# Seven products in place of eight for sixteen blocks of the down projection, and an opening in four parts, in a hybrid decoder step

## The chip, the cores and the metric

The kernel runs on one core of a Trainium2 chip. The time is that of one execution on the device, in microseconds (us); the profile adds one execution recorded instruction by instruction. The engines are PE (TensorE, matmuls), PEld (its weight load, which overlaps PE), DVE (VectorE), ACT (ScalarE), POOL (GpSimd) and SP (SyncE, which issues most DMAs). Each engine works through its own instructions in order, and semaphores make one wait for another.

## What is computed

One layer of a hybrid decoder for 1024 prompt tokens and 8 sample tokens, with 1024 channels: three mixers read the same normalized input through one combined projection, their outputs are merged into the residual, and a SwiGLU network with 2816 hidden channels follows. Cut to what matters here:

```python
xn = rmsnorm(x, norm_mix_w)
sc_b, sc_c, sc_x, z, xbc, dt_raw, q, gates = jnp.split(xn @ w_in, splits, axis=-1)
...
x = x + merged @ w_merge_o
hn = rmsnorm(x, norm_ffn_w)
x = x + (jax.nn.silu(hn @ w_ffn_gate) * (hn @ w_ffn_up)) @ w_ffn_down
y = rmsnorm(x, final_norm_w)
```

(The last lines are written here in short form.) Besides y, the step returns keys and values of the memory and the new convolution and state-space states.

## The kernel before

All activations lie channels by tokens: a tile is 128 channels by 1032 tokens (1024 prompt, 8 sample), and the halves of a tile are 516 tokens. Each number is split into a rounded high part and the rest (`hi` by a cast on ACT, `lo` by a subtraction on DVE), and a product is three matmuls: high·high, low·high, high·low. There are two ways to multiply. `gemm` (L183–206) takes a weight block of 128 columns against whole tiles in three pieces of 344 tokens. `strassen` (L290–350) takes two weight blocks at once and the input channels in two halves, and uses Strassen's identity: seven products of half-size operands in place of eight. For it the activations must lie in seven forms (B11, T1, nT2, B21, T3, B22, T4), each made of halves of the tiles by additions; the sums of weights are made by DVE per call. It works in three PSUM tiles of 516 tokens in two banks (m0, m1, m2), in matmuls of 258 tokens (L248). The products of a call come in the order B11, T1, nT2, B21, T3, B22, T4; a finished one is evacuated by an ACT copy (L318, L326, L329) or added by DVE (L331, L342, L344).

The program runs in stages on one core:

- **Opening** (L400–553): three groups of three token tiles (384 tokens; the last with the sample). For each group the mean square of each token (`square`, ACT), its root (`root_of`, DVE and PE), then per channel tile the transposes on PE into PSUM, an ACT copy to `xt` that SP stores to `xT_d` (the residual), the scaling on DVE into `xw`, and the split into `xn`. The products of the first two weight blocks (wB0, wC0) with a group run while the next group is prepared (`first_products` L500–502), and `step_sizes` gives dt. SP's queue carries, in this order: three token tiles, eight small parameter loads into `rows`, the weights wB0, wC0, wdt, the bias, the other token tiles.
- **z and Strassen forms**: two z blocks by `gemm`, the forms of xn (L1128–1145), then pairs of blocks by `strassen` (Z2 to Z14, G16, X17 to X19, and so on). Small work is put between products by a list `pend`, one entry per `tick`.
- **State-space scan, attention, output projections, merge** (untouched by the change).
- **Gate and up** (L1813–1845): the 22 hidden blocks in pairs (0, 1), (2, 3), and so on, each pair one `strassen` call for gate and one for up, then Silu and product, and SP stores each hidden tile to `h_d`.
- **Down** (L1869–1884): blocks 0–2, then 3–10, then 11–18 by `gemm`: `hidden` loads a tile of `h_d` and splits it, eight output tiles are computed per group, and DVE adds each to `x2[m]`, which was loaded from `x2_d` ahead. Blocks 19–21 belong to the finish, which goes token piece by token piece (L2003–2020) with the last norm and the output.

What stands on an engine's queue is decided by a scheduler that orders the instructions, by tile pools (a tile waits until the buffer that it takes is free), and by the few explicit `issue_after`.

## Time and profile before

| what | us |
|---|---|
| median of three timed runs | 2490.22 (2489.02 to 2492.35) |
| the profiled execution | 2485.14 |
| its span in the trace | 2483.4 |
| opening, to the first z product | 0 to 65.2 |
| last gate/up call (u20) | 2195.34 to 2215.6 |
| down projection, blocks 0 to 18 | 2216.44 to 2432.6 |
| finish | 2432.6 to 2483.4 |

The profiled execution lies 5.1 us below the median of the timed runs. In the opening PE is busy for 0.73 us of the first ten, then for 7.2, 7.5, 7.7 and 9.0 of each ten up to 50, and fully from there. To read rows of a timeline: start, duration, engine, line, operation, output<-inputs, shapes, and in brackets how long the engine was idle before it and what ended that.

### The profile page before, as it was taken

What the parts mean: (1) busy time and instruction counts of PE and PEld (TensorE: products, weight loads), DVE (VectorE), ACT (ScalarE), POOL (GpSimd) and SP (SyncE); (2) the same over time, 40 slices, a digit from 0 to 9 for tenths busy, and PEclk for the clock granted to TensorE, in tenths of its full rate; (3) what the DMA queues carried; (4) which work ended last, traced back from release to release, by engine and by line L of the source; (5) the groups of instructions that cost most, each with busy time, mean ns of one, the idle gap of its engine ahead of it and who ended that gap; (6) DMA issues with size and microseconds to landing.
All of it is one profiled execution on the core that took longest, in us unless ns stands there. A gap on an engine that the chain in (4) does not pass through costs nothing.

```text
span 2483.4 us, 44787 instructions
## 1 busy us (share of the span) xinstructions
PE 2442.8 (98%) x18691; PEld 2377.6 (96%) x18691; DVE 1505.5 (61%) x2434; ACT 1056.5 (43%) x1700; POOL 119.1 (5%) x163
## 2 busy tenths in 40 slices
PE   7999999999999999999999999999999999999998
PEld 5999999999999999999899988999999999999998
DVE  5744576786777676568677763555775544463315
ACT  5733554555453543656554442223443233341203
POOL 0200000000000000112211000000000000000000
PEclk9999999999999999999999999999999999999999
DMA  6444323444353345667886886855443222273211
GB/s 196 144 154 153 121 86 112 129 136 129 111 155 116 104 129 181 214 223 260 259 281 219 261 319 235 289 162 175 133 154 101 88 70 93 69 253 123 77 35 69
DMA packets 348474, 392.08 MB, mean 158 GB/s; under 512 B 15350, under 2 KB 285798, under 8 KB 348263
## 3 DMA queue, kind: packets, MB, share of 16 engines
q1 hardware_dynamic: 327678, 331.23, 42.6%
q10 hardware_dynamic: 20593, 57.97, 6.1%
q8 instruction: 147, 2.41, 0.4%
q14 instruction: 56, 0.46, 0.1%
HBM read 280.40 MB, written 108.98 MB: 157 GB/s over the span
## 4 chain that ended last, share of the span: by engine, by line
PE 89%; DMA 5%; DVE 3%; ACT 1%; issue 1%; SPq 0%; ACTq 0%; DVEq 0%; POOL 0%
PE po L203 11%; PE pd L203 9%; PE pm L1742 4%; PE ps_q L203 2%; PE pss L966 1%; PE py L953 1%; DMA qb<-qs_d 1%; PE X17m L248 1%; PE po L945 1%; PE ps_z L203 1%; PE Z2m L248 1%; PE G16m L248 1%; PE X4m L248 1%; PE X8m L248 1%; PE C7m L248 1%
## 5 line engine op out<-in xcount | busy, mean ns | idle before, releaser
L1884 DVE TENSOR_TENSOR x<-pd,x 128x1032 f32<-128x1032 f32 x24 | 29.5, 1231 | 129.3 <-PE pd L203 129.3
L898 ACT ACTIVATE r<-r,acum 128x128 f32<-128x128 f32 x256 | 78.9, 391 | 6.0 <-DMA r<-ac_d 5.5
L680 DVE SCALAR_TENSOR_TENSOR ax<-u,prm,ax 128x1024 f32<-128x1024 f32 x44 | 56.3, 1280 | 0.0
L839 ACT ACTIVATE st<-st,es 128x128 f32<-128x128 f32 x128 | 41.3, 392 | 24.8 <-DMA st<-in_state_ssm_dram 14.0
L930 POOL TENSOR_TENSOR xdd<-xdt,decst 128x512 f32<-128x512 f32 x32 | 36.2, 1131 | 280.3 <-DVE xdt L926 280.3
L924 DVE TENSOR_TENSOR r<-r,cbm 128x1024 f32<-128x1024 f32 x32 | 39.1, 1222 | 2.4 <-ACT r L899 0.4
L841 DVE SCALAR_TENSOR_TENSOR st<-sr,dts,st 128x128 f32<-128x128 f32 x128 | 40.0, 344 | 0.4
L949 DVE TENSOR_TENSOR y<-po,ea 128x512 f32<-128x512 f32 x28 | 19.3, 688 | 28.2 <-PE po L945 28.2
L845 DVE SCALAR_TENSOR_TENSOR sr<-st,sr 128x128 f32<-128x128 f32 x128 | 35.2, 284 | 1.1
L966 PE MATMUL pss<-xdd,bT 128*128 128x512 f32 x64 | 34.2, 616 | 1.1 <-ACT bT L923 0.9
L953 PE MATMUL py<-r,xdt 128*64 128x128 f32 x512 | 35.0, 279 | 0.0
L899 ACT ACTIVATE r<-r 128x1024 f32<-128x1024 f32 x32 | 33.9, 1058 | 0.6
L979 POOL TENSOR_TENSOR s<-s,cdec 128x512 f32<-128x512 f32 x28 | 33.1, 1183 | 2.6 <-DVE s L972 2.4
L1749 DVE TENSOR_TENSOR x<-pm,xT 128x516 f32<-128x516 f32 x16 | 11.1, 695 | 36.4 <-PE pm L1742 36.3
L1375 DVE TENSOR_TENSOR yr<-po,yr 128x1032 f32<-128x1032 f32 x8 | 9.8, 1231 | 38.2 <-PE po L203 38.2
L953 PEld LDWEIGHTS py<-r,xdt 128*64 128x64 f32 x512 | 27.3, 136 | 4.2 <-issue 0.6
L923 ACT COPY bT<-bp 128x128 f32<-128x128 f32 x32 | 8.5, 266 | 53.2 <-DVE cbm L921 53.0
L945 PE MATMUL po<-bc,s 128*128 128x128 f32 x224 | 29.8, 276 | 0.0
L945 PEld LDWEIGHTS po<-bc,s 128*128 128x128 f32 x224 | 28.2, 191 | 0.6 <-DVE s L972 0.4
L1476 DVE SCALAR_TENSOR_TENSOR kc<-kc,qb 128x256 f32<-128x256 f32 x64 | 23.5, 420 | 8.2 <-DMA qb<-qs_d 8.2
L1671 DVE TENSOR_TENSOR gt<-po,gt 128x1032 f32<-128x1032 f32 x8 | 9.9, 1231 | 30.7 <-PE po L203 27.1
L683 DVE SCALAR_TENSOR_TENSOR ax<-u,prm,ax 128x1032 f32<-128x1032 f32 x22 | 28.3, 1286 | 0.0
(9294 smaller groups left out, 8888.1 us busy)
## 6 DMA issues: line engine op xcount, KB each, us to landing
r<-ac_d SPq DMA_DIRECT2D x32, 512.0 KB
gt_d<-G ACTq DMA_DIRECT2D x24, 516.0 KB
gt<-gt_d SPq DMA_DIRECT2D x24, 516.0 KB
xs_d<-ax ACTq DMA_DIRECT2D x22, 516.0 KB
hr<-h_d SPq DMA_DIRECT2D x22, 516.0 KB
x<-xs_d SPq DMA_DIRECT2D x16, 516.0 KB
zs<-zs_d SPq DMA_DIRECT2D x16, 516.0 KB
yb_d<-x SPq DMA_DIRECT2D x16, 516.0 KB
```

What stands on the lines that cost most here:

```text
L203: PE.matmul(ps[:, n, :CW], wt[:, ks], x[:, n * CW : (n + 1) * CW], start=(k == 0 and i == 0), stop=(k == nk - 1 and i == 2),)
L248: PE.matmul(ps[:, n, :HC], wt[:, ks], x[:, n * HC : (n + 1) * HC], start=(start and kt == 0 and i == 0), stop=(kt == 3 and i == 2), skip_g ...
L680: V.scalar_tensor_tensor(acc[:, :T], u[:, j : j + T], w[j], acc[:, :T], op0=ALU.mult, op1=ALU.add)
L839: S.activation(st[:, i], st[:, i], AF.Copy, scale=es[:, g * 4 + i, b : b + 1])
L841: V.scalar_tensor_tensor(st[:, i], rb, dts[:, g * 4 + i, b : b + 1], st[:, i], op0=ALU.mult, op1=ALU.add)
L898: S.activation(r[:, j, :], r[:, j, :], AF.Relu, scale=-1.0, bias=acum[:, c, h : h + 1])
L924: V.tensor_tensor(r, r, bc(cbm.unsqueeze(1), [P, HPG, P]), op=ALU.mult)
L930: G.tensor_tensor(b3(xdd, HPG), b3(xdt, HPG), bc(decst[:, c, hs].unsqueeze(2), [P, HPG, 64]), op=ALU.mult)
L945: PE.matmul(po[:, t * P : (t + 1) * P], state["s"][:, t * P : (t + 1) * P], bcg[1][:, cs], start=True, stop=True,)
L953: PE.matmul(py[hp : hp + 64, (h // 2) * P : (h // 2 + 1) * P], xdt[:, h * 64 : (h + 1) * 64], r[:, (h % 2) * 4 + h // 2, :], start=True, s ...
L966: PE.matmul(pss, bT, xdd, start=True, stop=True)
L1742: PE.matmul(ps[:, n, :HC], wt[:, ks], x[:, half * HT + n * HC : half * HT + (n + 1) * HC], start=(k == 0 and i == 0), stop=(k == KD - 1 an ...
```

## The change

It has three parts.

**Down projection.** The hidden blocks are paired anew: (0, 9), (1, 5) to (4, 8), (11, 15) to (14, 18), (10, 19), (20, 21). For the eight pairs (j, j+4), DVE makes T1, T2, T3 and T4 right after the product of gate and up, and SP stores the seven half-width forms to `hf_d` in place of two tiles to `h_d`. In the down projection blocks 1–8 (part 0) and 11–18 (part 1) are then four `strassen` calls each (d00 to d06, d10 to d16), two output tiles a call. With `add=True`, `put` adds a finished product onto `x2` on DVE where ACT copied it. `st_begin` makes the weight sums of each part's first call ahead. Block 0 runs ahead of part 0, blocks 9 and 10 ahead of part 1, in halves of 516 tokens, in the same three PSUM tiles. Block 0's result is copied by ACT as the start of `x2`; the residual is loaded and added by ticks of part 0. The PSUM pool of `gemm` comes back only behind part 1.

**Opening.** Four parts of two token tiles (256, 256, 256 and 264 tokens) in place of three groups; channel tiles in the order 0, 4, 1, 5, 2, 6, 3, 7, two in one PSUM tile for the first three parts, so one evacuation of 512 columns for two; `xt` has four buffers and is stored from ACT's queue. The three weight loads follow the first two token tiles; the eight rows of the mixer norm are loaded apart from ACT's queue, the other parameters later. The square of the second tile is made by DVE. The accumulated first blocks leave PSUM in two pieces.

**Order between opening and gates.** T1 and nT2 of the forms are made before the z blocks, T4 after them; the convolutions of the two first blocks move from ahead of z into the call Z2 (`plain3`); the transposes of the memory become ticks; the first history becomes a tick of the z blocks and the other three come in the ticks of Z14, where two of them came in the last tick of G16; `bc_rows` becomes a tick.

```diff
+        def put(o, ps):
+            if add:
+                V.tensor_tensor(h3(o), hv(ps), h3(o), op=ALU.add)
+            else:
+                S.copy(h3(o), hv(ps))
...
-            S.copy(h3(o11), hv(pa))
+            put(o11, pa)
...
-        S.copy(h3(o22), hv(pb))
+        put(o22, pb)
...
-            S.copy(h3(o12), hv(pa))
+            put(o12, pa)
...
+        def tokens(g, ks):
+            n = parts[g][1]
+            ps = sm_ps(f"ps_xt{g}{ks[0]}")
+            for i, k in enumerate(ks):
+                turn(g, ps, i * n, lambda _, t, m: t[:, k * P : (k + 1) * P])
+            xt = p0.tile([P, 512], F32, tag="xt", bufs=4, name=f"xt{g}{ks[0]}")
+            S.copy(xt[:, : len(ks) * n], ps[:, : len(ks) * n])
+            to = xT_d[ks[0] :: 4] if len(ks) > 1 else xT_d[ks[0] : ks[0] + 1]
+            S.dma_start(to[:, :, part(g)].rearrange("k p t -> p k t"), b3(xt[:, : len(ks) * n], len(ks)))
+            for i, k in enumerate(ks):
+                ins = to_xn(g, k, ps[:, i * n : (i + 1) * n])
...
-    xbc_tile(16, "B0", ps_b0)
-    xbc_tile(20, "C0", ps_c0)
-    make_forms(0)
-    make_forms(2)
-    pend.extend([None, mem_rms])
+    mem_rms()
+    make_forms()
+    pend.extend([dt_turn, lambda: history("state_ssm_conv", h_xc, 16, ev_tile("hist", (24, D)))])
     z_step(0)
     z_step(1)
-    mem_block(0)
-    pend.extend([None, lambda: mem_block(1)])
+    make_forms4()
+    pend.extend([None, lambda: mem_block(0), lambda: mem_block(1)])
...
     def plain3():
         for kt in range(4):
             split_to(*xforms["T3"][kt], raw3[kt // 2][:, HS[kt % 2]])
+        xbc_conv(16, firsts[0], "B0")
+        xbc_conv(20, firsts[1], "C0")
...
+        V.tensor_sub(t1, b12, b11)
+        V.tensor_sub(t2, t1, b22)
+        V.tensor_sub(t3_, b22, b12)
+        V.scalar_tensor_tensor(t4, t2, -1.0, b21, op0=ALU.mult, op1=ALU.subtract)
+        for f, t in enumerate((b11, t1, t2, b21, t3_, b22, t4)):
+            SY.dma_start(hf_d[f, n - 1], t)
...
+    def down_pairs(part, fs, begun):
+        for m in range(0, KD, 2):
+            pa = strassen(
+                *down_src(part, m), fs, f"d{part}{m}", ev_sums,
+                lambda m=m: tuple(x2[m + i][:, c] for i in range(2) for c in HS), add=True,
+                begun=begun if m == 0 else None,
+            )
+            o21 = h3(x2[m + 1][:, HS[0]])
+            V.tensor_tensor(o21, o21, pa, op=ALU.subtract)
```

Three places show what moves. SP's queue at the program's start, before (x_ is a token tile, rows the parameter tile, wB0r to wdtr the raw weights):

```order
L405 DMA x_153<-in_x_prompt_dram 128x1024
L432 DMA rows<-in_norm_mem_w_dram 8x128
L432 DMA rows<-in_norm_mix_w_dram 8x128
L432 DMA rows<-in_norm_ffn_w_dram 8x128
L432 DMA rows<-in_sc_conv_w_dram 24x128
L432 DMA rows<-in_ssm_conv_b_dram 24x128
L432 DMA rows<-in_ssm_norm_w_dram 16x128
L432 DMA rows<-in_ssm_conv_w_dram 40x128
L432 DMA rows<-in_ssm_conv_w_dram 56x128
L124 DMA wB0r<-in_w_in_dram 128x8x128
L124 DMA wC0r<-in_w_in_dram 128x8x128
L124 DMA wdtr<-in_w_in_dram 128x8x128
```

The weight loads stand behind the third token tile and the eight parameter loads. The same queue after, from its first row:

```order
L428 DMA x_150<-in_x_prompt_dram 128x1024
L428 DMA x_152<-in_x_prompt_dram 128x1024
L124 DMA wB0r<-in_w_in_dram 128x8x128
L124 DMA wC0r<-in_w_in_dram 128x8x128
L124 DMA wdtr<-in_w_in_dram 128x8x128
L428 DMA x_160<-in_x_prompt_dram 128x1024
L428 DMA x_162<-in_x_prompt_dram 128x1024
L428 DMA x_164<-in_x_prompt_dram 128x1024
L428 DMA x_166<-in_x_prompt_dram 128x1024
```

The weights now stand behind two token tiles, and the parameters behind all of them. DVE at the first call of X17, before (ps_h is PE's transposed history, X17r the call's raw weights, sa, S and T its sums and their low parts):

```order
L660 COPY dts<-ps_ex 128x128
L661 COPY es<-ps_ex 128x128
L662 COPY dpar<-ps_ex 128x16
L550 COPY h_xc<-ps_h_8_3361 128x192
L550 COPY h_sc<-ps_h_0_3373 128x128
L315 TENSOR_TENSOR X17sa<-X17r_3422 128x512
L331 TENSOR_TENSOR u_3426<-X17m_3428,u_3426 128x516
L316 TENSOR_TENSOR X17sa<-X17sa,X17r_3420 128x512
L282 SCALAR_TENSOR_TENSOR X17sb<-X17sa,X17r_3420 128x512
L236 TENSOR_TENSOR X17Sl<-X17sa,X17Sh 128x1024
```

After, at the same place (the L754 and L757 rows are a convolution on 8 sample tokens):

```order
L736 COPY dts<-ps_ex 128x128
L737 COPY es<-ps_ex 128x128
L738 COPY dpar<-ps_ex 128x16
L337 TENSOR_TENSOR X17sa<-X17r_3504 128x512
L754 TENSOR_SCALAR ax_3709<-h_xc,prm 128x8
L338 TENSOR_TENSOR X17sa<-X17sa,X17r_3502 128x512
L757 SCALAR_TENSOR_TENSOR ax_3709<-h_xc,prm,ax_3709 128x8
L285 SCALAR_TENSOR_TENSOR X17sb<-X17sa,X17r_3502 128x512
L757 SCALAR_TENSOR_TENSOR ax_3709<-h_xc,prm,ax_3709 128x8
L239 TENSOR_TENSOR X17Sl<-X17sa,X17Sh 128x1024
```

The two history copies are gone from between dpar and X17sa. DVE where the first groups of the down projection begin, before (h7l to h10l are low parts of hidden tiles, wd02l to wd06l of weights, pd the PSUM tile of an output tile):

```order
L1866 TENSOR_TENSOR wd04l<-wd02r,wd04h 128x768
L1910 MEMSET fst 128x18
L163 TENSOR_TENSOR h7l<-hr_24146,h7h 128x1032
L163 TENSOR_TENSOR h8l<-hr_24152,h8h 128x1032
L1884 TENSOR_TENSOR x_0_23850<-pd_23872,x_0_23850 128x1032
L1884 TENSOR_TENSOR x_1_23852<-pd_23901,x_1_23852 128x1032
L1866 TENSOR_TENSOR wd06l<-wd03r,wd06h 128x768
L163 TENSOR_TENSOR h9l<-hr_24158,h9h 128x1032
L1884 TENSOR_TENSOR x_2_23854<-pd_23936,x_2_23854 128x1032
L163 TENSOR_TENSOR h10l<-hr_24164,h10h 128x1032
```

And after, at the first call d00 (B22, T3 and T4 with a digit pair are forms of part 0, d00r raw weights, L318 the adds of `put`, d00m PSUM tiles):

```order
L377 TENSOR_TENSOR T302al<-T_24195,T302ah 128x1032
L377 TENSOR_TENSOR B2200al<-B_24201,B2200ah 128x1032
L284 TENSOR_TENSOR d00sb<-d00r_24026,d00r_24028 128x512
L377 TENSOR_TENSOR B2202al<-B_24207,B2202ah 128x1032
L377 TENSOR_TENSOR T400al<-T_24213,T400ah 128x1032
L377 TENSOR_TENSOR T402al<-T_24219,T402ah 128x1032
L318 TENSOR_TENSOR x_0_24041<-d00m_24225,x_0_24041 128x516
L285 SCALAR_TENSOR_TENSOR d00sb<-d00sa,d00r_24026 128x512
L318 TENSOR_TENSOR x_1_24058<-d00m_24226,x_1_24058 128x516
L239 TENSOR_TENSOR d00Tl<-d00sb,d00Th 128x1024
L318 TENSOR_TENSOR x_0_24041<-d00m_24225,x_0_24041 128x516
L239 TENSOR_TENSOR d00Dl<-d00r_24028,d00Dh 128x512
```

In place of one add of a whole tile there are adds of halves, and the first of them stands behind the splits of the last forms.

More of the change, by code (lines that the diff above doesn't have):

```diff
@@ L434, in tile_kernel @@
                 at += m
-        ps = sm_ps("ps_prm")
-        for b in range(2):
-            PE.transpose(ps[:, b * P : (b + 1) * P], rows[:, b, :], ident)
-        V.tensor_copy(prm, ps[:, :208])
         def par(key, i):
             return prm[:, PC[key] + i : PC[key] + i + 1]
-        w_b0 = weights(wblock(w_in, C_XBC + 16 * P), "wB0")
-        w_c0 = weights(wblock(w_in, C_XBC + 20 * P), "wC0")
-        w_dt = load_raw(wblock(w_in, C_DT), "wdt")
         bias = cn.tile([P, 1], F32, tag="bias", name="bias")
@@ L460, in to_xn, with part, turn @@
+        def part(g):
+            c0, n = parts[g]
+            return slice(c0, c0 + n)
+        def turn(g, ps, at, of):
+            for i, (t, n) in enumerate(srcs[g]):
+                PE.transpose(ps[:, at + i * P : at + i * P + n], of(i, t, n), ident[:n, :n])
+        def to_xn(g, k, ps):
             hi, lo = xn[k]
-            xt = p0.tile([P, 384], F32, tag="xt", bufs=3, name="xt" + name)
-            S.copy(xt[:, :n], ps[:, :n])
-            SY.dma_start(xT_d[k, :, c], xt[:, :n])
+            c = part(g)
@@ new lines, in tile_kernel, with others, first_weights @@
+        order = (0, 4, 1, 5, 2, 6, 3, 7)
+        def others():
+            ps = sm_ps("ps_prm")
+            for b in range(2):
+                PE.transpose(ps[:, b * P : (b + 1) * P], rows[:, b, :], ident)
+            V.tensor_copy(prm[:, :200], ps[:, :200])
+        def first_weights(ins):
+            ws = []
+            for name in ("wB0", "wC0"):
+                raw = loaded.pop(name)
+                hi = wp.tile([P, 1024], F32R, tag="whi", name=name + "h")
+                in_turn("hi", S.copy(hi, raw))
+                ws.append((raw, hi))
+            for raw, hi in ws:
+                lo = wp.tile([P, 1024], F32R, tag="wlo", name="wl")
+                with tc.issue_after(ins):
+                    in_turn("lo", V.tensor_sub(lo, raw, f32(hi)))
+                yield hi, lo
@@ L497, in first_products @@
+        def first_products(g, k):
+            c, n = part(g), parts[g][1]
             ah, al = xn[k]
@@ L1898, in tile_kernel @@
+    pst_stack.close()
+    st_stack.close()
+    pmm[0] = ctx.enter_context(tc.tile_pool(name="pmm3", bufs=2, space=PSUM))
+    fin = ctx.enter_context(tc.tile_pool(name="fin", bufs=1))
+    js = list(range(19, 22))
+    for j in js:
+        hs[j] = hidden(j)
     wd = []
```

356 lines of the change are left out of this document (215 added, 141 removed).

## The prediction

> **What bounds the kernel now.** I read the page first: the busy times, the slices with the granted clock, the chain that ended last.
>
> ```profile
> span 2483.4 us, 44787 instructions
> PE   2442.8 (98%) x18691; PEld 2377.6 (96%) x18691; DVE 1505.5 (61%) x2434; ACT 1056.5 (43%) x1700; POOL 119.1 (5%) x163
> ...
> PEclk9999999999999999999999999999999999999999
> ...
> PE 89%; DMA 5%; DVE 3%; ACT 1%; issue 1%; SPq 0%; ACTq 0%; DVEq 0%; POOL 0%
> ```
>
> PE (TensorE) is busy for 98% of the span at a full granted clock, and the chain lies on PE for 89%. So there are two ways to gain: take products away from PE, or fill the 40 us in which it stands still. Where it stands still, the list of PE's waits says (line, what it waited for, total, times, longest):
>
> ```profile
> PE ps_prm L437 <- DMA rows<-in_ssm_conv_w_dram: 9.0, 1, 9.0
> PE ps_xt L481 <- DVE xw L465: 6.0, 4, 2.5
> ...
> PE X17m L248 <- ACT X17Sh L235: 2.6, 1, 2.6
> ...
> PE Z2m L248 <- ACT z L770: 1.2, 1, 1.2
> ...
> PE pd L203 <- DVE g20o L1843: 0.9, 1, 0.9
> ```
>
> The change touches each of these five places. In the chain, the end of gate and up and the down projection read so (start, duration, what):
>
> ```profile
> 2154.89 20.23 PE u18m L248 x168
> ...
> 2195.34 20.24 PE u20m L248 x168
> 2215.60 0.71 DVE g20o L1843
> 2216.44 216.12 PE pd L203 x1368
> ```
>
> A seven-product block is 168 matmuls of 258 columns in 20.23 us without a gap: 0.1204 us each. The down projection of blocks 0 to 18 is 1368 matmuls of 344 columns in 216.12 us: 0.158 us each. Both are limited by PE alone, so fewer columns are time.
>
> **Down projection, PE.** Eight blocks the old way are 8 blocks × 8 output tiles × 3 products × 3 column pieces = 576 matmuls, × 0.158 = 91.0 us. The new way is four seven-product calls, 4 × 20.23 = 80.9 us. Two such parts: 2 × (80.9 − 91.0) = **−20.2 us**. Blocks 0, 9 and 10 go in halves, 288 matmuls of 258 columns, × 0.1204 = 34.7 us, against 216 × 0.158 = 34.1: **+0.6**. The swap of PSUM pools moves behind part 1; it cost 0.9 us on L1843 and will cost about that again on the last subtraction: **0** (−0.9 to +0.9).
>
> **Down projection, what must keep up.** Evacuation moves from ACT copies to DVE adds, and forms are loaded rather than whole blocks. Rows nearest to the new operations:
>
> ```profile
> L1749 DVE TENSOR_TENSOR x<-pm,xT 128x516 f32<-128x516 f32 x16 | 11.1, 695 | 36.4 <-PE pm L1742 36.3
> L1884 DVE TENSOR_TENSOR x<-pd,x 128x1032 f32<-128x1032 f32 x24 | 29.5, 1231 | 129.3 <-PE pd L203 129.3
> ```
> ```profile
> 2103.34 0.69 DVE L236 TENSOR_TENSOR g16Dl<-g16r,g16Dh 128x512 fp32r<-128x512 f32 x1 [4.55 <-ACT g16Dh L235]
> ...
> 2113.03 1.22 DVE L236 TENSOR_TENSOR u16Sl<-u16sa,u16Sh 128x1024 fp32r<-128x1024 f32 x1
> ```
> ```profile
> 2097.15 0.59 ACT L318 COPY g16o<-g16m 128x516 f32<-128x516 f32 x1 [2.10 <-PE g16m L248]
> ...
> 2219.44 1.05 ACT L162 CAST h8h<-hr 128x1032 fp32r<-128x1032 f32 x1 [0.77 <-DMA hr<-h_d]
> ...
> 2229.25 1.06 ACT L162 CAST h9h<-hr 128x1032 fp32r<-128x1032 f32 x1 [3.64 <-DMA hr<-h_d]
> ```
>
> DVE per call: seven adds on 516 columns × 0.695 = 4.9; five operations on 512 columns × 0.69 = 3.5; three splits of 1024 × 1.22 = 3.7; together 12.0 us, in part 0 with two residual adds of 1032 × 1.23 = 14.5, of 20.23. It is not a bound by its sum. But DVE works in order, and the product that reuses a PSUM bank starts 5.78 us into a call (after B11 and T1, each 24 × 0.1204 = 2.89). At the start of the first call, three splits of forms (B22 of blocks 2 and 3, both T4) stand on DVE ahead of the first add, and the buffer of the first of them is free only as block 0's product ends. ACT then needs three casts × 1.05 = 3.15, the last split 1.23, the add 0.70, and on ACT one or two copies (0.59) come before: 5.1 to 6.3 us against 5.78, and the loads of these forms come late in a queue that already made h9 wait 3.64. I take **+1.2** (0 if all is early; 4.2 if the last form also waits for its load as h9 did: 6.3 + 3.64 − 5.78). In the other seven calls the adds are ready within 2.89 us: **0** (to 2.35 each, below). During block 0, ACT has 16 copies and four casts, 16 × 0.59 + 4 × 1.05 = 13.6 at face value, less as consecutive ACT rows overlap by about 0.1 (11.6), beside 96 × 0.1204 = 11.6 of PE: balanced, **0** (to +2, on the same bound).
>
> **Gate and up** get four DVE operations of 516 columns per pair, 2.8 us of a pair's 40.5, and store seven half pieces for two whole tiles. The row at 2103.34 shows DVE idle for 4.55 us within one block, so it is hidden: **0**; uncovered it would be 8 × 2.8 = 22. Within u20, ACT and DVE prepare block 0 and six form tiles where they prepared seven blocks: **0**.
>
> **Opening.** The row of the first cast and the rows that set the pace there:
>
> ```profile
> 11.98 1.04 ACT L152 CAST wB0h<-wB0r 128x1024 fp32r<-128x1024 f32 x1 [3.12 <-DMA wB0r<-in_w_in_dram]
> ...
> 14.20 0.61 DVE L465 SCALAR_TENSOR_TENSOR xw<-ps_xt,prm,rbc 128x384 f32<-128x384 f32 x1
> ...
> 15.43 0.64 PE L500 MATMUL ps_B<-xnh,wB0h 128*128 128x344 f32 x1
> ...
> 17.07 0.49 PE L502 MATMUL ps_B<-xnh,wB0l 128*128 128x344 f32 x1
> 17.36 0.49 PE L501 MATMUL ps_C<-xnl,wC0h 128*128 128x344 f32 x1
> ...
> 20.78 0.32 PE L500 MATMUL ps_B<-xnh,wB0h 128*128 128x344 f32 x1
> 20.94 0.32 PE L500 MATMUL ps_C<-xnh,wC0h 128*128 128x344 f32 x1
> ...
> 22.48 1.02 ACT L462 COPY xt<-ps_xt 128x384 f32<-128x384 f32 x2 [2.33 <-DMA xT_d<-xt]
> ...
> 23.66 0.55 PE L481 MATMUL ps_xt<-ident,x 128*128 128x128 f32 x3 [1.77 <-DVE xw L465]
> ...
> 65.20 0.73 PE L203 MATMUL ps_z<-xnh,wz0h 128*128 128x344 f32 x3
> ```
> ```profile
> 50.00:60.00 10.00, 10.00 (x68) 7.71 (x67) 6.49 (x16) 4.93 (x14) 0.00 (x0) 1.00 0.28 97
> ```
>
> The first product waits for wB0, whose load now stands ahead of the eight parameter loads in SP's queue and behind two token tiles instead of three (the 9.0 us of ps_prm lie in the same stretch, and the parameters but one are now needed a part later). Nothing in before shows the new arrival; from the wait of 3.12 alone it gains at least that where x and the root come no later, and by the shorter queue I take the first product at 11.5 instead of 15.43: **−4.0** (0 to −5). The evacuations waited for the stores of xt (2.33 us on ACT, 1.77 seen at PE); these go to ACT's own queue with four buffers: **−1.8** (0 to −3). In the last ten microseconds before 60 PE is full: 24 × 6 = 48 products of the last piece in a row, now 264 columns instead of 344. At 0.157 from start to start (20.78 to 20.94) these are 7.5 us; in proportion to columns 5.8: **−1.8** (0 to −2). Together **−7.6**, bounds 0 and −10. Between, ACT and DVE set the pace as before, since the columns that they copy, cast and scale are the same. ACT issues 20 stores itself now:
>
> ```profile
> 15.81 0.48 ACT L462 COPY xt<-ps_xt 128x384 f32<-128x384 f32 x1 [0.45 <-PE ps_xt L481]
> ...
> 112.62 0.33 ACTq L786 DMA_DIRECT2D zs_d<-Z  x1
> ```
>
> 20 × 0.33 = 6.6 us, beside 24 evacuations of 0.48 that become 20 of at most 0.59, and its last squares end before the last part: I take **0**, and the low bound of the gain holds it.
>
> **The waits at X17 and Z2.** DVE's timeline there:
>
> ```profile
> 311.60 0.36 DVE L550 COPY h_xc<-ps_h 128x192 f32<-128x192 f32 x1 [3.11 <-PE ps_h L549]
> 313.72 0.29 DVE L550 COPY h_sc<-ps_h 128x128 f32<-128x128 f32 x1 [1.76 <-PE ps_h L549]
> 313.93 0.68 DVE L315 TENSOR_TENSOR X17sa<-X17r 128x512 f32<-128x512 f32 x1
> ```
>
> X17's sums stand behind two history copies that wait for PE, 3.11 + 1.76. The histories now come a stage earlier and the sums follow the copy of dpar at once, so PE's 2.6 us go: **−2.6** (0 to −2.6). At Z2 the transposes of the memory fill the 1.2 us while z leaves PSUM: **−1.2** (0 to −1.2). What comes in there is DVE work: the two convolutions, T3 and T4 now all lie in Z2, 16 to 17 us of 20.23 with the block's own splits: I take **+0.6** (0 to 3, about two of its splits).
>
> **Sum:** −20.2 + 0.6 + 1.2 − 7.6 − 2.6 − 1.2 + 0.6 = −29.2. The profiled execution took 2485.14 us (span 2483.4); −29.2 gives 2455.9 for such a one. The three timed runs have a median of 2490.22, 5.1 above; from it, **2461.0**.
>
> **Rivals.** *The opening gains nothing* (20%). For it: smaller pieces are more scattered, and the first products run slow: at 17.07 and 17.36 they start 0.29 us apart, at 20.78 and 20.94 0.16, while PEclk reads full. If the scattered products stay at the slow pace through two parts, 96 products of 256 columns × (0.29 − 0.16) × 256/344 = 9.3 us are added, against the 7.6 gained: about nothing is left, and the time is 2461.0 + 7.6 = **2469**. Against it: the slow pace ended at 20.6 in before, with PE busy for only 7.2 of those 10 us.
> [...]
>
> *The adds stall the down projection* (15%). For it: DVE is in order, and splits in it wait for ACT up to 4.55 us (2103.34). An add behind such a wait comes 4.55 + 0.69 after its product; PE has 2.89 of cover: 5.24 − 2.89 = 2.35 lost, once in each of eight calls: 19 us back, **2480**; half of that 2471. Against it: DVE needs 12.0 to 14.5 of 20.23.
>
> *Slower than before* (3%): the same mechanism twice in a call, at the add into o22 and at that into o12: 8 × 4.7 = 37.6 us back, 2461.0 + 37.6 = **2499**. It decides from 29.2 / 8 = 3.65 us lost per call. Against it: ACT is rid of three copies of 0.59 in each call, so its casts come earlier than in gate and up, where 4.55 is the longest such wait of a block that lost nothing on PE.
>
> *The products don't get fewer* (1%), for instance if forms had to be reloaded by call: 2481. The order shows 168 matmuls per call.
>
> **How the numbers follow.** Forecast 61%: 2453 to 2467, from the terms' bounds that go together (opening −10 and no stall below; opening −4 and a first stall of 3 above). The first rival at 2469, half of the second at 2471 and its end at 2480 lie above. The range 2452 to 2472 leaves out the end of the second rival, the slower one and a little on the low side, together 2 in 10. A measurement of this kernel tells 0.2%, 5 us, from no change: slower than 2495 needs the third rival, 3%; within 2485 to 2495 come parts of the second and fourth, 3%; faster 94%.
>
> **What would show it.** Right: the profile of after has calls d00 to d16 at 20.2 us each in the chain, no PE wait on L318 of over 1 us except at d00, the first z product near 57, X17 without its wait. Wrong: PE waits on L318 or on casts of forms in every call; products in the opening still 0.2 us or more apart behind 25 us; a new wait at Z2's D split.

## The result and the profile after

| | before | after |
|---|---|---|
| median of the timed runs beside each other, us | 2491.28 (2489.02 to 2492.79, four runs) | 2472.62 (2469.34 to 2476.38, four runs) |
| the profiled execution, us | 2485.14 | 2469.34 |
| its span, us | 2483.4 | 2467.3 |

The ratio of after to before is 0.9929 (95% interval 0.9916 to 0.9942). So the kernel became faster, by 18.7 us at the medians and 16.1 us between the spans of the two traces, where 29.2 us were forecast. A second measurement of the unchanged new kernel, told below, gave a median of 2471.80 us.

The chain that ended last, at the end of gate and up and in the down projection, now reads so (start, duration, what):

```profile
2151.43 20.30 PE u10m L251 x168
...
2215.29 10.38 PE pd L2019 x78
2225.67 20.51 PE d00m L251 x168
2246.18 20.26 PE d02m L251 x168
...
2334.18 20.30 PE d10m L251 x166
2354.49 20.32 PE d12m L251 x168
2374.81 20.32 PE d14m L251 x168
2395.13 20.33 PE d16m L251 x168
2415.48 0.69 DVE x L1991
```

Blocks 0 to 18 of the down projection took from 2212.2 to 2416.2, 204.0 us for 216.0 before. The calls d00 to d16 stand in the chain, as forecast, each at little more than PE's own time. What is short lies between them: block 0, which ends at 2225.67, and blocks 9 and 10, which begin at 2307.61 and end before 2334.18. The list of PE's waits (line, what it waited for, total, times, longest):

```profile
PE ps_rb L495 <- DVE rst L104: 6.0, 1, 6.0
PE ps_B L565 <- ACT xnh L502: 4.0, 5, 1.7
...
PE ps_mix L445 <- DMA rmix<-in_norm_mix_w_dram: 2.4, 1, 2.4
PE ps_B L566 <- DVE xnl L503: 1.5, 3, 0.8
PE ps_q L203 <- ACT G L859: 1.3, 1, 1.3
PE pd L2019 <- DVE x L2025: 1.2, 2, 0.7
PE ps_xt L495 <- ACT xnh L502: 1.0, 2, 0.8
```

The 9.0 us of ps_prm, X17's 2.6 and the 6.0 of ps_xt on `xw` have gone. In place of the first stand 2.4 us for the norm's rows (ps_mix) and 6.0 for the first root (ps_rb); the first product starts at 12.73 instead of 15.43. In place of the waits on `xw` stand 6.5 us for the split of `xn` (casts `xnh` on ACT 5.0, subtractions `xnl` on DVE 1.5). And ps_q now waits for a gate.

Read by stages, from the first matmul of one to that of the next, the 16.1 us come out so:

| stage | before | after | difference | forecast |
|---|---|---|---|---|
| opening and first z blocks, to Z2 | 91.4 | 89.8 | −1.6 | −7.6 − 0.6 |
| Z2 to Z14 | 168.6 | 168.4 | −0.2 | 0 |
| Z14 to X0, with X17 in it | 113.7 | 108.4 | −5.3 | −2.6 |
| X0 to the first gate block (g0) | 1393.9 | 1396.4 | +2.5 | 0 |
| gate and up, to block 0 | 448.8 | 449.2 | +0.4 | 0 |
| down projection, blocks 0 to 18 | 216.0 | 204.0 | −12.0 | −18.4 |
| finish | 51.0 | 51.1 | +0.1 | 0 |

The swap of the PSUM pools, 0.9 us, lay in gate and up before and lies at the end of the down projection now. The first z product is a bad mark for the opening (65.2 before, 64.9 after), since the transposes ps_dtT, 2.0 us, now lie ahead of it and lay behind it before; so the stage is taken to Z2. Two terms carry the miss: opening and Z2 with 6.6 us and the down projection with 6.4. X17 gave twice what was forecast. Of the 1.6 us to Z2, 0.9 are the wait ahead of Z2 itself (1.17 us before, 0.25 after), so the opening alone gave 0.7.

How far such a table may be trusted, the other traces show. The attention stage, from ps_q to pm, is the same in every kernel here; it took 667.7 us before and 666.8 after, and 666.7 to 677.5 in the nineteen traces.

### The profile page after: what moved, and what is told of

The parts are those of the page before. It is cut to its first block, busy times and chain, and to the rows that moved or that the text cites. A ratio compares the mean times of both kernels' runs of the same rounds, so it can differ in the third digit from the quotient of the medians.

```text
span 2467.3 us, 45822 instructions
## 1 busy us (share of the span) xinstructions
PE 2428.0 (98%) x19020; PEld 2363.6 (96%) x19020; DVE 1602.1 (65%) x2606; ACT 1084.9 (44%) x1747; POOL 112.7 (5%) x163
## 5 line engine op out<-in xcount | busy, mean ns | idle before, releaser
L753 ACT ACTIVATE ax<-u,prm 128x1024 f32<-128x1024 f32 x22 | 27.4, 1246 | 1.4 <-DVE u L366 0.4
L1158 DVE SCALAR_TENSOR_TENSOR x<-x,prm,sqa 128x1032 f32<-128x1032 f32 x16 | 19.6, 1289 | 12.2 <-ACT sqa L1154 12.2
```

## The experiments

Some edits are shown against the kernel after, others against the one before; the text says which. Times of traces are start times in them.

### Each half alone

`e1_opening` is the change without its down projection, `e2_down` is the down projection alone. In lines, `e1` undoes

```diff
-        put(o22, pb)
+        S.copy(h3(o22), hv(pb))
...
-    hf_d = dram("hf_d", [7, 8, P, HT])
```

and what hangs on these; `e2` undoes the opening and the moved order:

```diff
-        parts = [(g * 256, 256 if g < 3 else 264) for g in range(4)]
-        places = (0, 256, 512, 1024)
...
+            xt = p0.tile([P, 384], F32, tag="xt", bufs=3, name="xt" + name)
+            S.copy(xt[:, :n], ps[:, :n])
+            SY.dma_start(xT_d[k, :, c], xt[:, :n])
```

> The kernel before with the new opening and the new order up to the gates, and with the old pairs and the old down projection. Theory A (each stage carries its own shortfall): the first z product starts at 64.9 us as in the profile of after, the X0 call about 7 us earlier than before, of which some 3 us are given back by the work that moved into the later calls, so the time is 4 us below the kernel before on the same chip (3 to 6). Theory B (the stages do what was forecast, and a slower clock beside the new down projection takes the rest): z at about 57 to 60, and 10 us below the kernel before.

> The kernel before with the new pairs and the new down projection, and with the old opening and order. Theory A: from the first product of block 0 to the first one of the finish 204 us as in after, where 216.1 plus the wait of 0.9 stood before, so the time is 12 to 13 us below the kernel before. Theory B: 197 to 199 us and 18 us below.

Measured: `e1` 2482.12 us (ratio 0.9974, 0.9961 to 0.9988), `e2` 2479.26 us (0.9961, 0.9948 to 0.9974), before beside them 2489.62. That is −7.5 and −10.4, together −17.9: the two halves add up to the change, and each is short of its own forecast (−10.8 with X17 and Z2 for the first, −18.4 for the second). Neither takes measurably from the other. `e1` falls between its two theories (z at 63.1 us, and 7.5 us gained with an interval of 3.0 to 9.7); `e2` lies near its theory A (12 to 13 us; 10.4 gained, 6.5 to 12.9). In `e2`'s own trace the down projection took 206.6 us, because block 0 took 17.3 there: PE waited 3.4 us for one ACT copy, and pairs of products were slow for 2.6 us behind it.

`e1` comes to Z2 at 88.0, before at 91.4 and after at 89.8. So of the 8.2 us that were forecast to that point 3.4 are there in `e1` and 1.6 in the trace of after, and the next views say why. Ten traces have this opening as it is in after. In the six whose clock stayed at 1.00 from 10 to 60 us, Z2 starts at 87.8 to 88.4; in the four others (after, `q3_order`, `r1_hold`, `r0_again`) at 89.4 to 94.8. The opening in stretches of ten microseconds (busy time of PE, PEld, DVE, ACT and POOL with their instructions, then granted clock, DMA share, GB/s), before:

```profile
20.00:30.00 10.00, 7.50 (x43) 5.83 (x42) 5.18 (x13) 5.21 (x14) 0.10 (x1) 1.00 0.52 188
30.00:40.00 10.00, 7.72 (x45) 5.87 (x44) 6.72 (x12) 7.29 (x16) 0.00 (x0) 1.00 0.72 219
40.00:50.00 10.00, 8.98 (x61) 6.55 (x62) 6.72 (x17) 6.46 (x15) 0.00 (x0) 1.00 0.50 155
```

and after:

```profile
20.00:30.00 10.00, 8.39 (x62) 7.25 (x62) 7.53 (x23) 7.02 (x16) 0.10 (x1) 1.00 0.61 172
30.00:40.00 10.00, 8.96 (x82) 7.88 (x80) 6.65 (x20) 6.52 (x16) 0.10 (x1) 1.00 0.52 168
40.00:50.00 10.00, 8.09 (x57) 5.69 (x57) 5.26 (x15) 6.07 (x14) 0.00 (x0) 0.85 0.35 107
50.00:60.00 10.00, 9.70 (x75) 7.56 (x75) 6.68 (x16) 6.51 (x17) 0.00 (x0) 0.98 0.30 103
```

PE is 0.9 to 1.2 us busier in each stretch from 20 to 40, yet there was little idle time to fill: before, PE stood still for 2.5 + 2.3 + 1.0 us between 20 and 50. And between 40 and 50 the granted clock of after is 0.85. The timeline of after there:

```profile
44.21 0.39 PE L565 MATMUL ps_B<-xnh,wB0h 128*128 128x256 f32 x1 [0.97 <-ACT xnh L502]
44.43 0.28 PE L565 MATMUL ps_C<-xnh,wC0h 128*128 128x256 f32 x1
45.50 0.39 PE L566 MATMUL ps_B<-xnl,wB0h 128*128 128x256 f32 x1 [0.79 <-DVE xnl L503]
...
46.88 1.93 PE L575 MATMUL ps_dt<-xw,wdtr 128*32 128x256 f32 x16
```

Two pauses of 0.97 and 0.79 us, and behind them the 16 small products of ps_dt take 1.93 us. In `e1` the same products take 1.07 us behind the same pauses, at a clock of 1.00. So whether such a pause costs again differs between executions of the same opening.

### What paces the opening

Five runs ask whether ACT's store issues, the order of loads, the slow first products or the split of wz0 hold the opening up. `e4_wz` (against after) splits the first z block's weights behind the second channel tile of the last part, where after splits them just ahead of that part, `p4_sp` gives the stores back to SP, `p5_loads` (against before) moves the loads alone, `p8_warm` and `q1_warm` put 26 and 12 matmuls on the identity (52 and 24 instructions in the trace) ahead of the first root:

```diff
+                if g == 3 and i == 1:
+                    loaded["wz0"] = load_raw(wblock(w_in, C_Z), "wz0")
...
-            S.dma_start(to[:, :, part(g)].rearrange("k p t -> p k t"), b3(xt[:, : len(ks) * n], len(ks)))
+            SY.dma_start(to[:, :, part(g)].rearrange("k p t -> p k t"), b3(xt[:, : len(ks) * n], len(ks)))
...
+        for col, name in ((16 * P, "wB0"), (20 * P, "wC0")):
+            loaded[name] = load_raw(wblock(w_in, C_XBC + col), name)
...
+        for i in range(26):
+            PE.matmul(ps[:, :P], ident, ident, start=True, stop=True)
```

> After, with the split of the first z weights placed behind the second channel tile of part 3; in after ACT and DVE make it between the last scaled tiles of part 2 and the first of part 3. Theory A (this split makes PE stand still from 43 to 45.5 us, and the pause then makes products slow until 50): both pauses go, the granted clock of the slice 40 to 50 us stays at 1.00, and the first z product starts at 60 to 62 in place of 64.9: 3 to 5 us. Rival (part 3 is late for the root of its tokens, whatever is split when): the pause stays between 43 and 50, and z starts at 64 or later.

> After, with the stores of the residual issued by SP again, the four buffers kept. Theory A (20 issues of 0.37 us on ACT delay the casts that PE waits for): PE's waits for the casts of xn (4.0 us in five) fall to 2 to 3, and the accumulation of the first blocks ends 1 to 2 us earlier than in the runs whose clock did not fall (61.1). Rival (ACT is not the chain; the buffers or the root of the next part are): the waits stay or those on stores come back, and it ends at 61 or later.

> The kernel before with its three groups, and only the loads in the new order: weights behind the first three token tiles, then the other tokens, the mixer norm apart on ACT's queue, the other parameters last. Theory A (the opening's gain is the earlier first product, and cutting it in four adds a boundary without work saved on PE): the first product starts at 12.5 to 13.5 us in place of 15.4, and the accumulation of the first blocks ends at 61 to 62.5, no later than with four parts. Rival (the smaller parts bring the gain): it ends at 63.5 or later.

> After, with 26 matmuls of the identity ahead of the first root, where PE stands still; their result is not used. Theory A (products of the first 3.5 us are slow because PE had done little before): the first products start 0.12 to 0.13 us apart where after has 0.21, and the last product of part 0 comes 1 to 1.5 us earlier; the pauses later on stay, so z starts 0 to 1.5 us earlier than in a run of after whose clock did not fall (62.9 to 63.3). Rival (the slow pace is of the first products as such, or of what feeds them): 0.21 stays.

> The changed kernel with 12 additional 128-column matmuls on the identity ahead of the first root (26 had delayed the first root by 4 us). Theory A: PE's activity ahead of the first products opens its clock, so these start 0.12 us apart and not 0.21, and since only 12 are put in, the root is delayed by at most 0.5: the first z product at 60 to 62, if no pause closes the clock again, against 61.1 to 62.9 of the changed kernel (its last product of the opening). The rival: the casts that PE waits for (about 4 us in the opening) set the pace, and z stays at 62.5 to 65 though the first products are faster.

| run | first product | first z product | what stood in its way |
|---|---|---|---|
| `e1_opening` | 12.51 | 63.1 | split of xn 6.4 us; no drop of the clock |
| after | 12.73 | 64.9 | split of xn 6.5 us; clock 0.85 in 40 to 50 |
| `e4_wz` | 12.69 | 68.2 | clock 0.50 in 54 to 62 |
| `p4_sp` | 12.53 | 67.1 | casts again 4.1 us; clock 0.66 in 50 to 60 |
| `p5_loads` (dt behind z) | 14.43 | 64.7 | 6.1 us on `xw`; clock 0.83 in 20 to 30 |
| `p8_warm` | 15.02 | 67.3 | the root 4 us later; clock 0.66 in 20 to 30 |
| `q1_warm` | 12.78 | 63.0 | split of xn 3.8 us; clock 0.87 in 10 to 20 |

`e4` timed at 2472.8 us (0.9932, 0.9912 to 0.9953). The others have a single execution each: `p4` 2478.46 us, `p8` 2471.71, `q1` 2467.24, and `p5` 2489.20 beside 2491.87 of the kernel before. `e4`'s edit did what theory A asked of the stretch from 40 to 50: the pause of 0.97 us is 0.58, that of 0.79 has gone, and the clock reads 1.00. But a pause came back later, and with it one of the two longest drops of the clock (the other is in `r0_again`: 0.50 from 50 to 60, 0.83 and 0.81 in the ten microseconds before and behind):

```profile
50.00:54.00 4.00, 3.07 (x15) 1.98 (x15) 3.36 (x7) 2.70 (x8) 0.00 (x0) 0.88 0.48 140
54.00:62.00 8.00, 8.00 (x41) 5.79 (x42) 5.09 (x11) 3.91 (x9) 0.00 (x0) 0.50 0.47 130
```

One pause of 0.90 us, which ends at 52.6, stands ahead of it, and then PE works for eight microseconds at a granted clock of 0.50. Giving the stores back to SP left the waits for casts where they were (4.1 for 4.0), so ACT's issues were not what held the casts up. The loads alone, with three token tiles ahead of the weights where after has two, bring the first product forward by 1.0 of the 2.7 us, to 14.43 where theory A had 12.5 to 13.5, and Z2 by 0.5 (90.9 for 91.4), with a clock of 0.83 in 20 to 30 that before does not have. What the loads alone give without such a drop stays open. The warm-up shows two things. In `p8` the matmuls ran until 12.7, past the point where the root was ready (8.63 in after). The root came 3.9 us later, the first product 2.3, and in 20 to 30 the clock read 0.66, with a pause of 2.4 us that ended at 21.2: it was too long. But its first products start 0.12 us apart, where after's start 0.21 apart up to 16.2 and 0.12 behind that: with matmuls ahead of them they were not slow. The granted clock of after reads 1.00 from 12 to 19, so the slow pace of the first products does not show in it. `q1` is short enough:

```profile
3.10 4.83 PE L587 MATMUL ps_warm<-ident 128*128 128x128 f32 x24
9.67 0.43 PE L495 MATMUL ps_rb<-ident,rst 128*128 128x128 f32 x2 [1.73 <-DVE prm L446]
...
12.78 0.38 PE L565 MATMUL ps_B<-xnh,wB0h 128*128 128x256 f32 x1 [1.50 <-ACT xnh L502]
13.00 0.28 PE L565 MATMUL ps_C<-xnh,wC0h 128*128 128x256 f32 x1
...
18.01 0.54 PE L565 MATMUL ps_B<-xnh,wB0h 128*128 128x256 f32 x1
18.35 0.41 PE L565 MATMUL ps_C<-xnh,wC0h 128*128 128x256 f32 x1
```

The first products come at the fast pace, some microseconds later 0.34 lie between two again, and z starts at 63.0, as in the undisturbed runs without any warm-up (`e1` 63.1, `e3_evac` 62.9, `p1_turn` 63.3). That is the rival's result: faster first products did not bring the end forward. It isn't a clean one, since the clock fell again behind them (0.87 in 10 to 20); that the split of `xn` and PE's own work set the end is argued, and no run took these waits away.

### X17 and the pause's second price

The windows of before around X17's wait, with the granted clock behind POOL's column:

```profile
314.00:318.00 4.00, 1.42 (x10) 1.21 (x10) 3.58 (x6) 3.35 (x7) 0.00 (x0) 0.94 0.05 9
318.00:322.00 4.00, 4.00 (x24) 4.00 (x24) 3.07 (x5) 0.36 (x1) 0.00 (x0) 0.63 0.64 157
322.00:326.00 4.00, 4.00 (x34) 3.84 (x33) 0.83 (x2) 2.13 (x3) 0.00 (x0) 1.00 0.32 95
```

and its timeline:

```profile
316.94 0.51 PE L248 MATMUL X17m<-T10ah,X17Sh 128*128 128x258 f32 x2 [2.58 <-ACT X17Sh L235]
317.29 0.42 PE L248 MATMUL X17m<-T10al,X17Sh 128*128 128x258 f32 x2
317.53 0.61 PE L248 MATMUL X17m<-nT20ah,X17Sh 128*128 128x258 f32 x2
317.94 0.63 PE L248 MATMUL X17m<-nT20al,X17Sh 128*128 128x258 f32 x2
```

Behind the wait of 2.58 us, pairs of matmuls start 0.43 us apart from 317.9 to 320.9, and 0.24 before and after it; in windows of one microsecond the clock reads 0.77 from 317, 0.50, 0.50 and 0.52 from 318 to 321, and 1.00 again from 321, some 3.4 us at 0.50. So the wait cost itself and some 1.7 us again. `p3_hist` moves the histories alone, in the kernel before:

```diff
-    pend.extend([dt_softplus, lambda: history("state_ssm_conv", h_xc, 0, wide("h0")), dt_sums])
+    pend.extend([
+        dt_softplus,
+        lambda: [history("state_ssm_conv", h_xc, 8 * i, wide(f"h{i}")) for i in range(2)],
+        lambda: [dt_sums(), history("state_conv", h_sc, 0, wide("h2")[:16])],
+    ])
     z_pair(14)
```

> The kernel before with nothing but the earlier histories (two of them and the sample's in the ticks of Z14). Theory A (the pause of 2.6 us at X17 costs a second time, since the granted clock stays near 0.6 for 3.4 us behind it): from the first product of Z14 to that of X18, 73.2 us before, it takes 68.0. Rival (only the wait goes, as forecast): 70.6.

From Z14 to X18 it took 69.4 us, for 73.2 before and 67.8 after: midway between theory A's 68.0 and the rival's 70.6. No wait of PE was left, but between 306 and 312 its clock was 0.74 on average, among the tiny transposes of ps_ex, and pairs of X17 started 0.43 apart from 309.7 to 311.8. Other traces settle it. With a drop at these transposes the stretch takes 74.6 us in the old order (`e2_down`, `p5_loads`) and 69.3 in the new one (`p2_pool`, `p4_sp`, `q3_order`, `r1_hold`); without it, 73.2 and 67.8. Like with like, the moved histories are worth some 5.3 us, which is theory A. And behind the wait of 2.6 us the clock from 318 to 322 is 0.62 or 0.63 in all three traces of the old order. `p3` ran once, at 2486.95 us beside 2490.44.

### The start of the down projection

`e3_evac` gives every second copy of block 0 to DVE; `q2_casts` issues the splits of part 0's last four forms behind block 0's last copy; `q3_order` does this and the like for two forms of part 1 (all against after):

```diff
+                elif half:
+                    V.tensor_copy(t, hv(ps))
```
```diff
-                    S.copy(t, hv(ps))
+                    last = S.copy(t, hv(ps)).ins
...
+                with nullcontext() if behind is None else tc.issue_after(behind):
+                    split_to(hi, lo, t[:, :TT].rearrange("p (k c) -> p k c", k=2))
...
+            hidden_forms(part, fs, NAMES[3:5])
+            hidden_forms(part, fs, NAMES[5:], last)
```

> After, with every second half of block 0 copied out of PSUM by DVE where ACT copied all. Theory A (ACT, with 16 copies and the casts of the forms in one queue, holds block 0 back): block 0's stretch falls from 13.4 to 11.7 us and the time by 1.5 against after. Rival (the forms' loads hold it back, or the splits in DVE's queue now delay its copies): 13.4 us or more, no gain.

> The changed kernel with one order changed: the casts and subtractions of part 0's last four forms (B21, T3, B22, T4) are issued behind block 0's last PSUM copy, where they stood ahead of or among its copies. Theory A: block 0 (96 matmuls, 11.6 us of work) took 13.4 us in the changed kernel because casts of forms stood ahead of copies on ACT; the stretch from its first product to that of call d00 now takes 11.7 to 12.2 us, and d00 to d10 stays at 107.4, since these forms are first needed 8.7 us into d00. The rival: the copies are the limit themselves (PE waits for the bank that ACT copies, as with the copies shared out): 13.4 again; or the forms are then late and d00 loses what block 0 gained: 12 and 109.

> As the kernel before it in this row, and also part 1's casts and subtractions of B22 and T4 are issued behind the last addition of blocks 9 and 10. Theory A: in the changed kernel blocks 9 and 10 took 25.4 us for 23.2 of matmuls because splits of forms stood ahead of additions on DVE; now 23.5 to 24.5, the waits of 0.56 and 0.65 on the additions are gone, and with block 0 the down projection takes 204.0 - 1.5 - 1.3 = 201.2 us; the time is 2 to 3 us below the changed kernel's, about 0.9985 of it at an opening with the same clock. The rival: the two forms are then late for d10, which waits 1 to 2 us on their subtractions: 204 again and the same time.

ACT's timeline in after, during block 0, which begins at 2212.17:

```profile
2212.75 1.05 ACT L376 CAST B2100ah<-B 128x1032 fp32r<-128x1032 f32 x1 [2.44 <-DMA B<-hf_d]
2213.71 1.04 ACT L238 CAST d00Sh<-d00sa 128x1024 fp32r<-128x1024 f32 x1
2214.65 1.57 ACT L2027 COPY x<-pd 128x516 f32<-128x516 f32 x3
2216.10 1.07 ACT L376 CAST B2102ah<-B 128x1032 fp32r<-128x1032 f32 x1
2217.05 2.29 ACT L2027 COPY x<-pd 128x516 f32<-128x516 f32 x4
```

Two casts stand ahead of the first copy and one ahead of each later group, and block 0 takes 13.5 us for 11.6 of matmuls. `e3` shares the copies out and gains nothing there: 14.8 us, with PE still waiting for ACT's half of the copies (1.8 us in three waits). It timed at 2471.7 us (0.9930, 0.9913 to 0.9946). `q2` and `q3` move the casts away, and block 0 takes 11.7 us in both. That shows the casts as the cause. But call d00 then waits; ACT and PE of `q3`:

```profile
2220.39 11.41 ACT L2028 COPY x<-pd 128x516 f32<-128x516 f32 x16
2231.70 1.06 ACT L376 CAST B2100ah<-B 128x1032 fp32r<-128x1032 f32 x1
...
2244.30 1.05 ACT L376 CAST T402ah<-T 128x1032 fp32r<-128x1032 f32 x1 [0.26 <-DMA T<-hf_d]
2246.00 1.04 ACT L238 CAST d00Th<-d00sb 128x1024 fp32r<-128x1024 f32 x1 [0.65 <-DVE d00sb L285]
```
```profile
2242.61 0.40 PE L251 MATMUL d00m<-B2102ah,d00Al 128*128 128x258 f32 x2
2247.10 0.80 PE L251 MATMUL d00m<-B2200ah,d00Th 128*128 128x258 f32 x2 [4.09 <-ACT d00Th L238]
2247.70 0.63 PE L251 MATMUL d00m<-B2200al,d00Th 128*128 128x258 f32 x2
```

The cast of d00's own third weight sum now stands behind all eight casts of forms, which wait for buffers and loads, and comes 4.1 us late; behind that pause the pairs again start 0.43 us apart for three microseconds. What block 0 gained, d00 gave back and more: the whole down projection took 208.8 us in `q2` and 205.9 in `q3`, for 204.0 in after and 201.2 expected. `q2`'s single execution was 2476.14 us, `q3` 2475.91 (0.9936, 0.9919 to 0.9953). The second half of the rival was right, the first of theory A.

### The splits of part 1's forms

`p2_pool` gives the subtractions of T3 and T4 in part 1 to POOL; `p6_noforms` uses part 0's forms once more in part 1, and for blocks 9 and 10 too, so that none of these is loaded or split; it leaves out the product of these ten blocks:

```diff
+                if part and name in ("T3", "T4"):
+                    S.copy(hi, src)
+                    G.tensor_sub(lo, src, f32(hi))
...
-        hidden_forms(part, fs, NAMES[3:])
+            hidden_forms(part, fs, NAMES[3:])
```

> After, with the low parts of the T3 and T4 forms of part 1 made by POOL (GpSimd) in place of DVE. Theory A (DVE's queue between parts 0 and 1 holds PE: splits of forms stand ahead of the adds that empty PSUM): the stretch of blocks 9 and 10 falls from 25.4 us and more to at most 24.3, and the wait ahead of the first product of part 1 (0.8) goes. Rival (a late load or ACT's cast holds the same adds, or POOL's work slows DVE's): 25 us or more.

> After, with no forms loaded or split for part 1: part 1 and blocks 9 and 10 multiply the forms of part 0 in their place, so the product of those ten blocks is left out, with the same matmuls and evacuations. Theory A (the splits of part 1's forms, in order with the adds on DVE, cost PE its pauses there): the stretch of blocks 9 and 10 takes 23.3 us where after has 25.4, the wait of 0.8 ahead of part 1 goes, and so do the waits in d06. Rival (the 16 adds alone, with two PSUM tiles ahead, are too slow for PE): 25 us.

`p6` takes 105.0 us from d00 to d10, 2.4 less than after's 107.4, and 60.8 from d10 to d16 for 61.9; the whole down projection 200.8 for 204.0. PE's waits for DVE in blocks 9 and 10 are all but gone (0.2 for 1.2). So part 1's loads and splits cost 3.2 us against this trace of after, though DVE has idle time in that stretch (in after it is busy for 23.6 of the 26.6 us of blocks 9 and 10 to d10). Against the six traces of programs that differ from after in the opening alone or not at all (after, `e4`, `p4`, `p8`, `q1`, `r0`: 202.0 to 204.0 us) they cost 1.2 to 3.2. DVE in after shows how:

```profile
2313.13 1.98 DVE L2025 TENSOR_TENSOR x<-pd,x 128x516 f32<-128x516 f32 x3
2317.47 1.23 DVE L377 TENSOR_TENSOR B2110al<-B,B2110ah 128x1032 fp32r<-128x1032 f32 x1 [2.36 <-ACT B2110ah L376]
2318.62 0.69 DVE L2025 TENSOR_TENSOR x<-pd,x 128x516 f32<-128x516 f32 x1
```

The addition of 2318.62 stands behind a split that waits 2.36 us for its cast (whose load ended at 2316.4 in the chain). `p2` (2473.20 us, once) made this worse: 109.4 us from d00 to d10, 3.6 us of PE waiting for DVE, since DVE now waited for POOL to free a buffer:

```profile
2331.12 0.69 DVE L284 TENSOR_TENSOR d10sb<-d10r,d10r 128x512 f32<-128x512 f32 x1 [4.18 <-POOL T410al L1975]
2332.33 2.34 DVE L285 SCALAR_TENSOR_TENSOR d10sb<-d10sa,d10r 128x512 f32<-128x512 f32 x1
```

In `q3`, with B22 and T4 held back, blocks 9 and 10 took 24.0 us (2318.84 to 2342.83) for 25.4 and d10 had no wait: theory A for this part, though one wait of 0.6 on an addition stayed.

### The pace of the calls

A seven-product call takes 20.30 us in gate and up of after, 20.23 before, with the same 168 matmuls. `e1`, `e3` and `p4` have 20.30, `e2` and `p3` 20.23: the pace goes with the program. By the order in which buffers are taken, `e1`, which has no new down projection, should have after's placement of the forms in memory; no view shows the places. `p1_turn` reserves one place of `ah` and two of `al` ahead of gate and up, so that its forms of T1 and nT2 lie elsewhere; `p9_both` is this with the 26 matmuls of `p8`:

```diff
+    for tag, n in (("ah", 1), ("al", 2)):
+        for i in range(n):
+            G.memset(act_tile(tag, f"skip{tag}{i}", F32)[:, :1], 0.0)
```

> After, with three small buffer reservations ahead of the merge, which give the T1 and nT2 forms of gate and up other places in SBUF and change no product. Each seven-product call takes 20.30 us in after and with the opening alone, and 20.23 in before and with the down projection alone, and the former two share their places of forms and weights, and so do the latter two. Theory A (the place of the forms decides): the calls of gate and up take something other than 20.30, most likely 20.23 to 20.28. Rival (something else of the program, as the places of the weights, decides): 20.30.

> The matmuls of p8_warm and the reservations of p1_turn together on after, as the version that may beat both kernels. If the two gains are real they add 1 to 3 us: 2469 to 2471 as median against 2472.6 of after, which the timing can hardly tell; by the rival that the single run of p1_turn was only one with a clock that did not fall: 2472 or more.

The gate and up calls of `p1` take 20.27 us and d02 20.21 for 20.26, while the earlier calls stay as they were. So the place of the forms does act on the pace, by half of the difference in gate and up; by what mechanism, no run shows. `p1`'s single execution took 2464.48 us, with an opening whose clock never fell; `p9`, timed, came to 2473.13 (0.9936, 0.9919 to 0.9952), no better than after: its opening began later by the matmuls.

### Both of the better edits together

`r1_hold` joins `p1`'s reservation with the half of `q3` that helped (part 1's B22 and T4 behind the last addition; part 0 as in after). `r0_again` is the kernel after, unchanged, beside it.

> The changed kernel once more, unchanged, as the comparison for the next run: 2469 to 2476 us, from run to run by the opening's clock.

> The changed kernel with two edits that earlier runs point to: part 1's splits of B22 and T4 behind the last addition of blocks 9 and 10 (the stretch took 24.0 us in place of 25.4 and d10's wait of 0.76 went), and the forms of gate and up at other addresses (16 calls 0.03 us shorter each, d calls 0.1). Theory A: both hold, 2.2 + 0.5 + 0.8 = 3.5 us below the changed kernel run beside it, whose median lies some 0.14% higher. The rival: the forms are late for d10, or the addresses give their gain back elsewhere: within 1 us of it.

Six executions of each: `r0` 2471.80 us (2465.84 to 2475.72; 0.9922, 0.9904 to 0.9939), `r1` 2466.82 (2463.09 to 2474.05; 0.9911, 0.9896 to 0.9927). The median is 5.0 us lower, but the intervals overlap, and the two profiled executions are alike (2474.79 and 2474.05), so a gain of `r1` over after isn't proved. In its trace the edits do what they were to: 20.27 us a call in gate and up, d12 at 20.27 for 20.32, no wait at d10, and 201.3 us for the down projection. `r0`'s own trace has 202.0 there where the first trace of after had 204.0; DVE's wait for the cast of B2110 was 0.67 us and not 2.36. So of the down projection's shortfall some 2 us vary from execution to execution.

`r0`'s trace also tells how lucky the first trace of after was elsewhere: its opening lost 4.9 us (z at 69.8 for 64.9), with a clock of 0.50 from 50 to 60, and the attention stage, from ps_q to pm, took 670.5 us for 666.8.

## Why the prediction was partly wrong

**Direction and kind: right.** Products that are saved on a bound PE came back as time (−12.0 us in the down projection); the calls d00 to d16 stand in the chain at PE's own pace, and X17's wait is gone. The time, 2472.6, lies 11.6 us above the forecast of 2461.0 and 0.6 above the range. That it came so near to the range is luck: X17 gave 2.7 us more than forecast, for a reason that the prediction didn't have, and this hid a part of the misses elsewhere.

**The opening (with Z2 −8.2 forecast, −1.6 in the trace, −3.4 undisturbed): the step that failed.** "Together −7.6" added three gains as if each moved the end. The first product did come earlier, by 2.7 us, not 4.0. PE's work up to Z2 stayed nearly the same, so a gain there had to come out of its idle time. From 10 to 60 us that went from 8.6 to 6.9 us (`e1` 6.6), and from 0 to 10 from 9.3 to 8.4: 2.5 to 2.9 us in all, of which the slow clock of after's trace took part back. The third term, 7.5 to 5.8 us for a last piece of fewer columns, took no work away, since the columns taken from the last part went to the others. (Its "24 × 6 = 48" should read 8 × 6; the 7.5 us are right.) For the second, the stores of `xt`, the waits of 6.0 us on `xw` did go, but 6.5 us for the split of `xn` came in their place: ACT and DVE "set the pace as before", the prediction said, and that sentence spoke against its own sum. That these waits keep the rest of the gain is argued; no run took them away. The rival on the opening gave about the right size by another mechanism: the products did not stay slow, but new waits took the place of old ones, and their pauses now and then cost clock (0 in six traces, 1 to 7 us in four).

**X17 (−2.6 forecast, −5.3 measured): the wait right, its price too small.** The wait was priced at its own 2.6 us; the trace of before showed some 1.7 us of the rest, pairs at 0.43 instead of 0.24 for three microseconds with a granted clock of 0.63 from 318 to 322, and the prediction looked only at the idle time. What the last 1.0 us is, no view shows.

**The down projection (−18.4 forecast, −12.0 measured, −14.0 in `r0`'s trace): the other step that failed; costs set at nothing were not nothing.** "Balanced, 0 (to +2)" for block 0 was the upper bound, +1.9: the casts' sum was right, their place ahead of the copies was not asked. Blocks 9 and 10 with d10 took 46.9 us (2307.61 to 2354.49) for 23.1 + 20.23: +3.5 (1.9 less from d06 to d12 in `r0`'s trace), a place at which the prediction counted no form splits at all, though it had counted them for d00. `q2`, `q3` and `p6` show both causes. The calls' slower pace and the last subtraction add about 1.1, d06's wait 0.6. The stall that was priced, +1.2 at d00, was 0.3. The adds in the other calls cost nothing but d06's wait: the second rival did not come.

**Z2:** its wait fell from 1.2 to 0.2 us, nearly as forecast, and the +0.6 for DVE's new work didn't come.

**The middle (0 forecast, +2.5):** no term was written for it. PE got four waits that before did not have (ps_q 1.3, G8 0.7, X12 0.5, X8 0.4: 2.9), and a slower pace of its calls. They lie between X0 and ps_q, 633.7 us for 630.2. The two halves tell where they come from: `e1` has the waits at ps_q (1.3) and G8 (0.8) and takes 632.4, `e2` has neither and takes 630.6. So they came with the opening and the moved order; which of its moves made them stays open. The other 1.0 us, gained behind ps_q, lies within what the attention stage varies by.

## What to carry to other kernels

Before adding gains of one stage, count how much of the bound engine's time is idle there, say for each gain which idle time it removes, and ask what the engine will wait for next: work that only moves to another part is no gain (three terms summed to −7.6 us here, and the opening alone gave −0.7). Price a wait of the TensorE by the granted clock behind it as well as by its length (X17: 2.6 us, and some 1.7 more at a clock of 0.50), and read that clock in windows of some microseconds: over 62 us, the length of a slice of the page, X17's reads 0.97 (310 to 372 in before). Where an engine takes on new work, ask for each group of it what stands ahead of it in that engine's order, at every place where the group recurs: holding work back frees what stood behind it, and makes late what comes after (`q3`: block 0 took 11.7 us for 13.5, and a cast of d00 came 4.1 us late).

## What the runs showed of the hardware

- A pause of TensorE between 0.8 and 2.6 us was followed in some executions by two microseconds and more at half pace (X17 in before: behind 2.58 us, pairs 0.43 us apart for 0.24 from 317.9 to 320.9, clock 0.63 from 318 to 322; `e4`: behind 0.90 us, clock 0.50 from 54 to 62), and in others not: `e1` has after's pauses of 0.97 and 0.79 us, and its 16 products of ps_dt behind them took 1.07 us where after's took 1.93. The pauses of 3.4 us (`e2`) and 4.1 us (`q3`) were each followed by slow pairs, for 2.6 and some 3 us. What decides it for the short pauses, no run shows.
- The clock also fell without a pause of PE, among tiny transposes: `p3`, 0.74 from 306 to 312 us with no wait on PE's list, and 1.00 there in before and after.
- The same 168 matmuls took 20.19 (`e2`'s d02) to 20.33 us (after's d16), and other places of the forms in memory went with a change of 0.03 to 0.05 us (`p1`: 20.27 for 20.30 in gate and up, d02 20.21 for 20.26).
- In `p2` a SCALAR_TENSOR_TENSOR of 512 columns with both tensors in SBUF, begun 0.6 us into a POOL subtraction of 2.40 us, took 2.34 us where after has 0.69. A TENSOR_TENSOR with one input in PSUM, begun together with the same subtraction, kept its 0.69.
